# A hybrid attention and state-space block: PE's instruction order gets a rule on the kind of product, and attention's output gates are computed between heads and kept in DRAM

## The chip, the cores and the metric

The kernel runs on one core of a Trainium2 chip. The metric is device time in microseconds (us), the median of several executions. The core's engines are PE (matrix products), DVE (vector work), ACT (activations and copies), POOL, and SP, which here only issues transfers.

## The reference, cut to what matters

One encoder layer over 512 rows and 16 meta rows (L = 528), width 1024. Everything starts from one input projection; an attention branch of 16 heads and a state-space branch (SSD, 4 groups of 8 heads) run beside each other and are mixed by two gates.

```python
u = rmsnorm(h, norm_w[l])
proj = u @ w_in[l]
q_lat, kv_lat, k_rope, g_attn, z, xbc, dt_raw, merge = jnp.split(proj, offsets, axis=-1)
y_a = mla_branch(q_lat, kv_lat, k_rope, cos, sin, ...)        # 16 heads of softmax(q k^T) v
y_a = (y_a * jax.nn.silu(g_attn)) @ w_attn_proj[l]
y_s = ssd_branch(z, xbc, dt_raw, ...)                          # two directions, chunks of 128
y_s = y_s @ w_ssd_proj[l]
gates = jax.nn.sigmoid(merge).reshape(Bz, L, N_BRANCHES, D_MODEL)
mixed = gates[:, :, 0] * y_a + gates[:, :, 1] * y_s
h = h + mixed @ w_out[l]
h = rmsnorm(h, final_norm_w)
```

All inputs are float32. `gates[:, :, 0]`, the gate on attention's output, needs only `u` and 1024 columns of `w_in`.

## The kernel before, in words

The work is cut into small generators (units). A unit of the input projection loads a weight block of 1024 x 128 (512 KB, tile `wr`), ACT casts it to the high part `wh`, DVE makes the low part `wl`, and PE adds 24 products of 128x512 (or 48 of 128x270) into a PSUM tile `pj`: eight of high by high, eight of high by low, eight of low by high. That is the fp32r kind of product, one pass each. The SSD products (`st`, `yo`, `yd`, `cb` and a few more) take plain float32 operands, which PE runs as two recorded instructions each; the code calls these `four`. Transposes (`tr`, `yt`, `pt`) do not count as `four`.

PSUM has four one-bank tiles of tag "m" and two two-bank tiles of tag "d". The conv tiles of SSD, the products `yo`, attention's scores `sc` and keys take a "d" tile; each is handed back by DVE or ACT when it has been read.

Two steps set the order. First `drive` runs the units (main ones, and a queue of fillers, each with a condition) and records every operation with its place. Then `_Recorder.order` emits the operations by list scheduling: each engine has a clock, each operation an estimated length, and of all operations whose inputs are there the one with the earliest start, and among equals the one with the lowest place (`rank`), goes next. Each engine executes its own list strictly in that order. When PE goes from `four` to the other kind or back, this planner adds `SWITCH` = 95 ns.

```python
if o.eng == "PE" and o.four != four:
    four, more = o.four, self.SWITCH
```

For a head pair p of attention the queue holds the query and key units (`qst`, `kst`), values (`v`), the merge gate of the state-space branch (`merge_s`, tiles `ms`), and the branch gate `g` (`silu_tile`, tiles `z`). For a head, `score_gen` makes the scores `sc` in four row tiles; DVE takes the maximum `mx`, ACT the exponential `p`, DVE the reciprocal `sm` and the scaling; `value_gen` transposes (`pt`), splits into high (ACT) and low (DVE) parts `pT`, and multiplies with `v` into `o`. `split_y` splits the gated result `y` into `yah` and `yal`.

Attention's output gate is `merge_a(m)`, eight units of 24 products, each followed by one tanh on ACT into a tile `ma` of [128, 512]. Before, all eight may start when head 13 is done (`GATES` = 13), their tiles stay in SBUF, and `mix_unit(m)` uses them: it multiplies `ysp` (all eight split `y`) with `w_attn_proj`, then takes gate and sum. Behind the mixes come the last products `wo`.

Of the kernel before, what the change touches and what calls it, by code (L numbers as in the profile page):

```python
# [9 lines left out]
F32 = mybir.dt.float32  # L10
# [6 lines left out]
P = 128  # L17
# [26 lines left out]
LAG = 1250.0  # L44
MAHEAD, TOKC, CBC = 2, 2, 1
MAINS, OPEN, LOOK = 24, 4, 20
QLATE, GATES, SPLIT = 1, 13, 99


WPOOL, WPOOLB = 2, 4  # L50
# [41 lines left out]
class _Recorder:  # L92
# [15 lines left out]
    @classmethod  # L108
    def region(cls, ap):
        step = ap.ap[0][0]  # L110
        if ap.name == "cum_rows":
            return 0, 1, [(0, 1)]
        p0, f0 = divmod(ap.offset, step) if step else (0, ap.offset)
        dims = [(st, n) for st, n in ap.ap[1:] if st and n > 1]
        if "PSUM" in str(getattr(ap, "space", "")):
            end = f0 + sum(st * (n - 1) for st, n in dims)
            return 0, P, [(f0 // cls.BANK * cls.BANK, (end // cls.BANK + 1) * cls.BANK)]
        dims.sort(reverse=True)
        spans = [(f0, f0 + 1)]
        for k, (st, n) in enumerate(dims):  # L120
            rest = sum(a * (b - 1) for a, b in dims[k:]) + 1
            inner = sum(a * (b - 1) for a, b in dims[k + 1:]) + 1
            if inner >= st or n * len(spans) > 32:
                return p0, p0 + ap.shape[0], [(a, a + rest) for a, _ in spans]
            spans = [(a + st * m, a + st * m + 1) for a, _ in spans for m in range(n)]
        return p0, p0 + ap.shape[0], spans
# [31 lines left out]
        o.tiles = sorted({n for n, _ in rs + ws if n in self.tags})  # L158
        self.ops.append(o)

    AHEAD, SPARE = 4, 2
    TO_PE, TO_REST, SWITCH = 155.0, 35.0, 95.0

    def order(self):


        ops = self.ops
        left, ready = [0] * len(ops), [0.0] * len(ops)
        for o in ops:
            o.succs = []  # L170
        for o in ops:
            for k in o.preds:
                ops[k].succs.append(o)
            left[o.i] = len(o.preds)
        count, last, held, place, turn, passed = {}, {}, set(), {}, {}, {}
        for o in ops:
            for n in o.tiles:
                if n not in count:
                    tag = self.tags[n]
                    place[n] = turn.get(tag, 0)  # L180
                    turn[tag] = place[n] + 1
                count[n] = count.get(n, 0) + 1
        turn = {t: 0 for t in turn}
        passed = {t: set() for t in turn}
        free = {t: [0.0] * self.cap[t] for t in turn}
        clk = {e: 0.0 for e in ("PE", "DVE", "ACT", "POOL", "SP")}
        cand = {e: [] for e in clk}
        port = lock = wire = 0.0
        four = False
        for o in ops:  # L190
            if not left[o.i]:
                cand[o.eng].append(o)

        def when(o):
            t = max(clk[o.eng], ready[o.i], lock if o.eng == "POOL" else port if o.both else 0.0)
            for n in o.tiles:
                if n not in held:
                    tag = self.tags[n]
                    f, ahead = free[tag], place[n] - turn[tag]
                    if not f or ahead > self.AHEAD or (ahead > 0 and len(f) <= self.SPARE):  # L200
                        return None
                    t = max(t, f[0])
            return t

        out = []
        while len(out) < len(ops):
            best = None
            for q in cand.values():
                for o in q:
                    t = when(o)  # L210
                    if t is not None and (best is None or (t, o.rank) < best[:2]):
                        best = (t, o.rank, o)
            if best is None:
                raise RuntimeError(("no operation can go", len(out)))
            t, _, o = best
            cand[o.eng].remove(o)
            o.start = t
            for n in o.tiles:
                if n not in held:
                    held.add(n)  # L220
                    tag = self.tags[n]
                    free[tag].pop(0)
                    passed[tag].add(place[n])
                    while turn[tag] in passed[tag]:
                        turn[tag] += 1
            more = 0.0
            if o.eng == "PE" and o.four != four:
                four, more = o.four, self.SWITCH
            elif o.both:
                lock = t + o.occ  # L230
            elif o.eng == "POOL":
                port = t + o.occ + 60.0
            if o.eng == "SP":
                clk["SP"] = t + 420.0
                wire = max(wire, t + 1600.0) + o.dur
                end = wire + o.extra
            else:
                clk[o.eng] = t + o.occ + more
                end = t + o.dur + more
            for n in o.tiles:  # L240
                last[n] = max(last.get(n, 0.0), end + 40.0)
                count[n] -= 1
                if not count[n]:
                    f = free[self.tags[n]]
                    f.append(last[n])
                    f.sort()
            for s in o.succs:
                to = end + (self.TO_PE if s.eng == "PE" else self.TO_REST) if s.preds[o.i] else t + o.occ
                ready[s.i] = max(ready[s.i], to)
                left[s.i] -= 1  # L250
                if not left[s.i]:
                    cand[s.eng].append(s)
            out.append(o)
        self.span = max(o.start + o.dur for o in out)
        return sorted(out, key=lambda o: (o.start, o.i))
# [98 lines left out]
def hybrid_block_kernel(ctx, tc, a, out):  # L354
    nc = tc.nc
    scr = nc.dram_tensor("cum_rows", (2, NC, 32, P), F32, kind="Internal").ap()

    cp = ctx.enter_context(tc.tile_pool(name="cp", bufs=1))
    rp = ctx.enter_context(tc.tile_pool(name="rp", bufs=WRAW))
# [438 lines left out]
    def has(*keys):  # L798
        return lambda: all(k in done for k in keys)
# [468 lines left out]
    def merge_s(m):  # L1268
        w = yield from w_cols(O_MS + m * P)
        ps = yield from proj(w, u_src, QRY)  # L1270
        wdone()
        yield
        z = slot([P, NX], name="ms")
        A.activation(z, ps, AF.Tanh, scale=0.5)
        drop("m")
        yield
        V.scalar_tensor_tensor(ysacc[:, m, :], z, 1.0, ysacc[:, m, :], op0=ALU.add, op1=ALU.mult)
        done.add(("ms", m))

    w_ap = a["w_attn_proj"][0].rearrange("(k p) m -> p k m", p=P)  # L1280
    mx_, gates, ysp = {}, {}, {}

    def merge_a(m):
        w = yield from w_cols(O_MA + m * P)
        ps = yield from proj(w, u_src, QRY)
        wdone()
        yield
        z = slot([P, NX], name="ma")
        A.activation(z, ps, AF.Tanh, scale=0.5)
        drop("m")  # L1290
        gates[m] = z
        done.add(("ga", m))

    def split_y(p):
# [7 lines left out]

    def mix_unit(m):
        w = yield from weights(lambda raw: [(raw, w_ap[:, :, m * P:(m + 1) * P])], KD, P)
        ps = yield from proj(w, [ysp[p] for p in range(KD)], slice(0, NX))
        wdone()
        yield has(("ga", m), ("ms", m))
        z = gates.pop(m)
        V.scalar_tensor_tensor(z, z, 1.0, ps, op0=ALU.add, op1=ALU.mult)
        drop("m")  # L1310
        tt(V, z, z, ysacc[:, m, :], ALU.add)
        yield
        h = slot([P, NX], F32R, name="mxh")
        l = slot([P, NX], F32R, name="mxl")
        A.copy(h, z)
        yield
        lo_of(V, l, z, h)
        mx_[m] = (h, l)
        done.add(("mx", m))
# [117 lines left out]
    def fill(makes, cond=None):  # L1437
        for mk in makes:
            queue.append(Item(mk, cond))
# [85 lines left out]
    for p in range(KD):  # L1525
        if p % 2 == 0:
            fill([lambda p=p: pe_unit(p // 2)], lambda p=p: lat_ok() and score_ok(2 * p - 3))
        fill([lambda p=p: q_unit(p), lambda p=p: k_unit(p)], lambda p=p: "att" in done and lat_ok() and score_ok(2 * p - 2))
        if p % 2 == 0:
            fill([lambda p=p: v_unit(p // 2)], lambda p=p: lat_ok() and (p == 0 or ("A", 2 * p - 3) in done))  # L1530
        if p == 0:
            proj_fill(3)
        fill([lambda p=p: merge_s(p)], lambda p=p: ("proj", 3, p // 2) in done)
        if p + 1 < KD:
            g_fill(p + 1)
    fill([lambda m=m: merge_a(m) for m in range(KD)], lambda: ("A", GATES) in done)
    for h in range(NH):
        main(lambda h=h: score_gen(h), lambda h=h: ("q", h) in done and ("k", h) in done
             and (h < 1 or ("P", h - 1) in done) and (h < 2 or ("A", h - 2) in done))
# [47 lines left out]
```

## Time and profile before

| | |
|---|---|
| median of 3 runs | 912.46 us (910.71 to 915.15) |
| the profiled execution, its own time | 913.33 us |
| its span, first to last instruction | 911.5 us |
| PE busy | 878.5 us, 96% of the span |
| DVE busy | 707.9 us, 78% |
| ACT busy | 543.2 us, 60% |
| PE's idle time | 33 us |

Busy time of PE is the union of its matrix products; weight loads run beside them (PEld). The span falls into the start (to 25 us), the state-space groups (to about 500 us), attention's heads (to about 804 us), the mixes with the last products (to about 907 us) and the final rows. All work on `L261` is recorded by one helper, so instructions are told apart by their tiles.

### The profile page before, as it was taken

The page shows a single profiled execution, that of the slowest core. Times are in us where ns is not written, and L with a number is a line of the kernel's source. Part 1 is how long each engine was busy: PE and PEld are TensorE (multiplying, and loading weights), DVE is VectorE, ACT ScalarE, POOL GpSimd, SP SyncE. Part 2 cuts the span into 40 slices and gives each one's busy share as a digit, 9 for nine tenths or more (in the row PEclk, how much of TensorE's full clock was granted, in tenths as well). Part 3 has the DMA queues.
Part 4 walks back from the last instruction along what each step waited for, and adds up shares of the span by engine and source line. Part 5 has one row for each costly group of instructions (what it writes and reads, how often), then busy time and mean ns, then how long its engine had stood idle before and what let it go on. Part 6 is the DMA issues. An engine that isn't in the chain of part 4 may idle for free.

```text
span 911.5 us, 13243 instructions
## 1 busy us (share of the span) xinstructions
PE 878.5 (96%) x4984; PEld 725.7 (80%) x4984; DVE 707.9 (78%) x1245; ACT 543.2 (60%) x1159; POOL 11.7 (1%) x20
## 2 busy tenths in 40 slices
PE   7999999999989999999999999999999999999997
PEld 5997878867878769977788888877777878888885
DVE  6798799968799689979768757969989897334464
ACT  6369469965776447855344556757777685432232
POOL 1000000000000000000001000000000000000000
PEclk9999999999999999999999999999999999999998
DMA  7254246434524236332224333121121001433322
GB/s 219 71 165 119 70 120 166 109 93 113 141 70 139 70 84 160 104 116 70 70 70 102 81 87 92 38 53 29 38 50 33 15 24 47 135 121 101 104 70 92
DMA packets 126952, 83.30 MB, mean 91 GB/s; under 512 B 26354, under 2 KB 114071, under 8 KB 126889
## 3 DMA queue, kind: packets, MB, share of 16 engines
q1 hardware_dynamic: 126709, 82.33, 33.3%
q8 instruction: 39, 0.64, 0.3%
q14 instruction: 24, 0.20, 0.1%
q10 hardware_dynamic: 180, 0.14, 0.0%
HBM read 80.22 MB, written 2.23 MB: 90 GB/s over the span
## 4 chain that ended last, share of the span: by engine, by line
PE 74%; DVE 17%; ACT 4%; issue 2%; DMA 1%; POOL 0%; POOLq 0%; ACTq 0%; DVEq 0%
PE pj L261 53%; PE wo L261 4%; PE sc L261 3%; PE st L261 2%; PE yo L261 2%; PE o L261 2%; DVE x L261 2%; DVE wl L261 2%; PE pt L261 2%; PE tr L261 2%; PE yd L261 1%; DVE mx L261 1%; DVE pT L261 1%; DVE yo L261 1%; DVE C L261 1%
## 5 line engine op out<-in xcount | busy, mean ns | idle before, releaser
L261 PE MATMUL pj<-uh,wh 128*128 128x512 f32 (+3 forms) x776 | 158.8, 346 | 8.0 <-DVE yo L261 3.5
L261 DVE TENSOR_TENSOR wl<-wr,wh 128x1024 fp32r<-128x1024 f32 (+1 forms) x102 | 123.9, 1217 | 53.2 <-ACT wh L261 53.0
L261 PE MATMUL pj<-uh,wl 128*128 128x270 f32 (+3 forms) x776 | 157.1, 339 | 0.0
L261 PE MATMUL pj<-ul,wh 128*128 128x270 f32 (+3 forms) x776 | 150.0, 335 | 0.0
L261 ACT CAST wh<-wr 128x1024 fp32r<-128x1024 f32 (+1 forms) x102 | 106.3, 1042 | 63.1 <-PE pj L261 41.3
L261 PEld LDWEIGHTS pj<-uh,wh 128*128 128x128 f32 (+1 forms) x776 | 121.9, 191 | 27.6 <-issue 5.1
L261 PEld LDWEIGHTS pj<-ul,wh 128*128 128x128 f32 (+1 forms) x776 | 122.6, 189 | 15.0
L261 PEld LDWEIGHTS pj<-uh,wl 128*128 128x128 f32 (+1 forms) x776 | 122.0, 190 | 13.2 <-issue 0.2
L261 ACT ACTIVATE ar<-ar,nacs 128x128 f32<-128x128 f32 x256 | 80.8, 391 | 24.5 <-DMA ar<-cum_rows 19.3
L261 PE MATMUL sc<-kst,qst 96*128 96x264 f32 (+1 forms) x384 | 67.2, 299 | 6.3 <-ACT p L261 5.4
L261 PEld LDWEIGHTS sc<-kst,qst 96*128 96x128 f32 (+1 forms) x384 | 53.6, 189 | 11.7 <-ACT p L261 8.6
L261 ACT ACTIVATE p<-sc,mx 128x528 f32<-128x528 f32 x64 | 45.3, 707 | 21.3 <-DVE mx L261 20.8
L261 PE MATMUL pt<-cst,p 128*128 128x128 f32 (+1 forms) x320 | 52.2, 274 | 1.4 <-DVE pT L261 0.8
L261 DVE TENSOR_TENSOR pT<-pt,pT 128x512 fp32r<-128x512 f32 x64 | 43.8, 685 | 11.5 <-ACT pT L261 11.3
L261 PE MATMUL o<-pT,v 128*128 128x512 f32 x128 | 46.6, 417 | 3.5 <-ACT pT L261 2.9
L261 DVE SCALAR_TENSOR_TENSOR x<-pj,chv,x 128x528 f32<-128x528 f32 x64 | 48.8, 763 | 0.8 <-ACT x L261 0.3
L261 PEld LDWEIGHTS pt<-cst,p 128*128 128x128 f32 (+1 forms) x320 | 37.3, 130 | 12.7 <-DVE p L261 1.5
L261 DVE TENSOR_REDUCE mx<-sc 128x1 f32<-128x528 f32 x64 | 44.6, 698 | 2.2 <-PE sc L261 1.9
L261 ACT CAST pT<-pt 128x512 fp32r<-128x512 f32 x64 | 37.3, 587 | 14.6 <-PE pt L261 14.4
L261 ACT ACTIVATE w<-cbm,dt_t 128x128 f32<-128x128 f32 x128 | 39.9, 390 | 2.9 <-DVE cbm L261 2.9
L261 PE MATMUL pj<-nh,wh 128*128 128x512 f32 x128 | 39.6, 431 | 0.0
L261 DVE SCALAR_TENSOR_TENSOR w<-cbm,dt_t,w 128x128 f32<-128x128 f32 x128 | 38.1, 347 | 0.0
(224 smaller groups left out, 1467.2 us busy)
## 6 DMA issues: line engine op xcount, KB each, us to landing
wr<-in_w_in SPq DMA_DIRECT2D x69, 512.0 KB, 4.0
ar<-cum_rows SPq DMA_DIRECT2D x32, 512.0 KB, 5.3
wr<-in_w_ssd_proj SPq DMA_DIRECT2D x16, 512.0 KB, 3.4
wr<-in_w_attn_proj SPq DMA_DIRECT2D x8, 512.0 KB, 3.6
wr<-in_w_out SPq DMA_DIRECT2D x8, 512.0 KB, 3.7
ws<-in_w_uq SPq DMA_DIRECT2D x36, 64.0 KB, 3.3
xt<-in_x SPq DMA_DIRECT2D x4, 512.0 KB, 5.3
fin<-in_x SPq DMA_DIRECT2D x4, 512.0 KB, 6.0
```

What stands on the lines that cost most here:

```text
L261: o.fn(*o.args, **o.kw)
```

## The change: what it does

There are two parts. In `order`, a PE operation of the other kind than the one PE last ran gets 30 added to its place when candidates with the same start are compared (`STAY`). And `merge_a(p - 1)` is queued with head pair p, to start when head 2p-1 is done (the last one when head 14 is done); its tile goes to DRAM (`gate_rows`) by a transfer on SP's queue, and `mix_unit` loads it back into a tile `ga` before its products.

```diff
-QLATE, GATES, SPLIT = 1, 13, 99
+QLATE, SPLIT = 1, 99
...
-    AHEAD, SPARE = 4, 2
+    AHEAD, SPARE, STAY = 4, 2, 30
...
                     t = when(o)
-                    if t is not None and (best is None or (t, o.rank) < best[:2]):
-                        best = (t, o.rank, o)
+                    if t is None:
+                        continue
+                    r = o.rank + (self.STAY if o.eng == "PE" and o.four != four else 0)
+                    if best is None or (t, r) < best[:2]:
+                        best = (t, r, o)
...
+    gate_scr = nc.dram_tensor("gate_rows", (KD, P, NX), F32, kind="Internal").ap()
...
     def merge_a(m):
         w = yield from w_cols(O_MA + m * P)
...
         z = slot([P, NX], name="ma")
         A.activation(z, ps, AF.Tanh, scale=0.5)
         drop("m")
-        gates[m] = z
+        yield
+        S.dma_start(gate_scr[m], z)
         done.add(("ga", m))
...
     def mix_unit(m):
         w = yield from weights(lambda raw: [(raw, w_ap[:, :, m * P:(m + 1) * P])], KD, P)
+        yield has(("ga", m))
+        z = slot([P, NX], name="ga")
+        S.dma_start(z, gate_scr[m])
         ps = yield from proj(w, [ysp[p] for p in range(KD)], slice(0, NX))
         wdone()
-        yield has(("ga", m), ("ms", m))
-        z = gates.pop(m)
+        yield has(("ms", m))
...
         fill([lambda p=p: merge_s(p)], lambda p=p: ("proj", 3, p // 2) in done)
+        if p:
+            fill([lambda p=p: merge_a(p - 1)], lambda p=p: ("A", 2 * p - 1) in done)
         if p + 1 < KD:
             g_fill(p + 1)
-    fill([lambda m=m: merge_a(m) for m in range(KD)], lambda: ("A", GATES) in done)
+    fill([lambda: merge_a(KD - 1)], lambda: ("A", NH - 2) in done)
```

The order that comes out differs on PE, DVE, ACT and SP from about the second state-space step on. PE's list shows it at three places (the number behind a name is its buffer, the same tile may have another number in the other kernel).

The first place is PE's list at the beginning of the first state-space group; `st` are the float32 products of the states. Before:

```order
L261 MATMUL st_225<-xw_224,bt_193 128x512
L261 MATMUL tr_227<-cst,x_81_185 16x128 x4
L261 MATMUL pj_237<-uh,wh_230 128x512 x8
L261 MATMUL pj_237<-uh,wl_231 128x512 x4
L261 MATMUL st_238<-xw_235,bm_198 128x512
L261 MATMUL tr_240<-cst,x_81_185 128x128 x4
L261 MATMUL pj_237<-uh,wl_231 128x512 x4
L261 MATMUL pj_237<-ul,wh_230 128x512 x8
L261 MATMUL st_243<-xw_242,bt_193 128x512
L261 MATMUL tr_245<-cst,x_81_185 128x128 x4
```

The same place in the change:

```order
L266 MATMUL tr_227<-cst,x_81_185 16x128 x4
L266 MATMUL st_225<-xw_224,bt_193 128x512
L266 MATMUL pj_237<-uh,wh_230 128x512 x8
L266 MATMUL pj_237<-uh,wl_231 128x512 x4
L266 MATMUL tr_240<-cst,x_81_185 128x128 x4
L266 MATMUL pj_237<-uh,wl_231 128x512 x4
L266 MATMUL pj_237<-ul,wh_230 128x512 x8
L266 MATMUL tr_245<-cst,x_81_185 128x128 x4
L266 MATMUL pj_249<-uh,wh_233 128x270
L266 MATMUL st_238<-xw_235,bm_198 128x512
L266 MATMUL st_243<-xw_242,bt_193 128x512
```

The second and the third `st` have moved behind the transposes and the rest of the unit, and stand together.

The second place is PE's list between two heads in the middle of attention, beginning within the scores of one row tile. Before:

```order
L261 MATMUL sc_1230<-kst_812,qst_811 128x264
L261 MATMUL o_1192<-pT_1214,v_1134 128x512
L261 MATMUL sc_1230<-kst_812,qst_811 128x264 x4
L261 MATMUL o_1192<-pT_1214,v_1134 128x512
L261 MATMUL pt_1234<-cst,p_1201 128x128 x2
L261 MATMUL pt_1226<-cst,p_1212 128x128
L261 MATMUL pt_1234<-cst,p_1212 128x128
L261 MATMUL sc_1236<-kst_812,qst_811 128x264 x3
L261 MATMUL o_1192<-last_821,v_1145 128x512
L261 MATMUL sc_1236<-kst_812,qst_811 128x264 x3
```

The matching place in the change, where `pj_1257` is a unit of `merge_a`:

```order
L266 MATMUL sc_1251<-kst_812,qst_811 128x264 x3
L266 MATMUL o_1211<-pT_1232,v_1162 128x512
L266 MATMUL sc_1251<-kst_812,qst_811 128x264 x3
L266 MATMUL pj_1257<-uh,wh_1252 128x512 x2
L266 MATMUL pt_1247<-cst,p_1234 128x128
L266 MATMUL pj_1257<-uh,wh_1252 128x512 x2
L266 MATMUL o_1211<-last_821,v_1166 128x512
L266 MATMUL pj_1257<-uh,wh_1252 128x512 x3
L266 MATMUL pt_1247<-cst,p_1234 128x128
L266 MATMUL pj_1257<-uh,wh_1252 128x512
L266 MATMUL pj_1257<-uh,wl_1253 128x512 x4
```

The holes between transposes, scores and `o` now have the products of a gate unit in them.

The third place is PE's list where the last head ends. Before, with `pj_1402` and `pj_1415` as units of `merge_a`:

```order
L261 MATMUL pj_1402<-uh,wh_1391 128x512 x8
L261 MATMUL pj_1402<-uh,wl_1392 128x512 x4
L261 MATMUL o_1384<-pT_1398,v_1252 128x512 x2
L261 MATMUL pt_1403<-cst,p_1359 16x128 x2
L261 MATMUL pt_1403<-cst,p_1372 16x128 x2
L261 MATMUL pj_1402<-uh,wl_1392 128x512 x4
L261 MATMUL pj_1402<-ul,wh_1391 128x512 x8
L261 MATMUL o_1384<-pT_1400,v_1255 128x512 x2
L261 MATMUL o_1384<-last_821,v_1266 128x512
L261 MATMUL pj_1415<-uh,wh_1405 128x512 x8
L261 MATMUL pj_1415<-uh,wl_1406 128x512 x8
```

The same place in the change, where `pj_1430` is the first mix and waits for `yah`:

```order
L266 MATMUL o_1399<-pT_1406,v_1275 128x512 x2
L266 MATMUL pt_1410<-cst,p_1384 128x128 x2
L266 MATMUL pt_1410<-cst,p_1395 128x128 x2
L266 MATMUL pt_1412<-cst,p_1384 16x128 x2
L266 MATMUL pt_1412<-cst,p_1395 16x128 x2
L266 MATMUL o_1399<-pT_1408,v_1287 128x512
L266 MATMUL pj_1430<-yah_1350,wh_1423 128x512
L266 MATMUL o_1399<-pT_1408,v_1287 128x512
L266 MATMUL o_1399<-pT_1411,v_1296 128x512
L266 MATMUL pj_1430<-yah_1352,wh_1423 128x512
L266 MATMUL o_1399<-pT_1411,v_1296 128x512
L266 MATMUL pj_1430<-yah_1354,wh_1423 128x512
```

The gate units behind the last head are gone; the first mix begins with the seven `yah` that are ready.

## Rows read from the trace of the kernel before

**Rows 1.** The page: busy time, and the granted clock in 40 slices.

```profile
PE 878.5 (96%) x4984; PEld 725.7 (80%) x4984; DVE 707.9 (78%) x1245; ACT 543.2 (60%) x1159; POOL 11.7 (1%) x20
...
PEclk9999999999999999999999999999999999999998
```

**Rows 2.** Busy time by stage; columns: stretch, its length, each engine's busy time (instructions).

```profile
110.00:500.00 390.00, 382.38 (x2235) 311.22 (x2234) 335.99 (x567) 245.99 (x563) 6.54 (x7) 1.00 0.39 105
500.00:560.00 60.00, 60.00 (x314) 50.59 (x312) 40.22 (x74) 32.19 (x63) 0.00 (x0) 1.00 0.35 87
560.00:760.00 200.00, 188.01 (x1144) 157.72 (x1143) 174.94 (x356) 144.99 (x311) 0.00 (x0) 1.00 0.18 40
760.00:880.00 120.00, 120.00 (x550) 97.71 (x549) 55.05 (x74) 41.95 (x62) 0.00 (x0) 1.00 0.32 101
```

**Rows 3.** PE's waits: us in total, times, longest.

```profile
PE sc L261 <- ACT p L261: 5.4, 9, 1.4
PE pj L261 <- DVE yo L261: 3.5, 2, 2.0
...
PE pj L261 <- DVE x L261: 2.8, 2, 2.1
...
PE nwb L261 <- DMA nw<-in_norm_w: 2.2, 1, 2.2
```

**Rows 4.** The chain that ended last, 200 to 232 us: start, us, what.

```profile
200.97 1.73 PE yo L261 x4
...
209.89 1.02 PE yd L261 x16
210.92 1.91 PE yo L261 x4
212.83 2.78 PE pj L261 x12
215.61 0.86 PE st L261 x2
...
216.90 5.57 PE pj L261 x24
222.47 0.59 PE yd L261 x8
...
231.11 1.05 PE st L261 x2
```

**Rows 5.** Busy time in six stretches between heads, with their sum.

```profile
567.00:573.10 6.10, 4.54 (x30) 3.65 (x30) 6.10 (x14) 4.47 (x11) 0.00 (x0) 1.00 0.00 0
...
730.00:736.40 6.40, 4.96 (x28) 3.15 (x26) 6.20 (x14) 5.49 (x14) 0.00 (x0) 1.00 0.32 82
sum 38.70, PE 29.48 PEld 22.20 DVE 37.72 ACT 31.15 POOL 0.00; mean PE 4.91 PEld 3.70 DVE 6.29 ACT 5.19 POOL 0.00
```

**Rows 6.** Busy time in a stretch with a gate `g` as filler.

```profile
658.00:668.00 10.00, 9.43 (x51) 7.62 (x51) 7.12 (x16) 5.66 (x14) 0.00 (x0) 1.00 0.01 2
```

**Rows 7.** Busy time during PE's wait at 116 us and just after it.

```profile
116.10:118.10 2.00, 0.02 (x1) 0.00 (x0) 2.00 (x5) 0.33 (x2) 0.00 (x0) 1.00 0.66 149
118.10:121.90 3.80, 3.80 (x18) 3.80 (x19) 3.80 (x7) 0.61 (x1) 0.00 (x0) 0.55 0.88 260
```

**Rows 8.** The timeline where the last head ends: start, us, engine, what.

```profile
798.36 1.23 DVE L261 TENSOR_TENSOR wl<-wr,wh 128x1024 fp32r<-128x1024 f32 x1 [3.03 <-ACT wh L261]
...
804.42 0.39 PE L261 MATMUL o<-last,v 128*128 128x512 f32 x1
...
805.72 0.58 ACT L261 COPY y<-o 64x512 f32<-64x512 f32 x1
...
806.99 0.69 DVE L261 TENSOR_TENSOR y<-o,y 64x512 f32<-64x512 f32 x1
...
808.44 0.62 ACT L261 CAST yah<-y 128x512 fp32r<-128x512 f32 x1 [2.14 <-DVE y L261]
```

**Rows 9.** Transfers by line: count, KB each, median us to landing.

```profile
out<-fo SPq DMA_DIRECT2D x8, 256.0 KB, 2.2
```

More of the change, by code (lines that the diff above doesn't have):

```diff
@@ L112, in region @@
             return 0, 1, [(0, 1)]
+        if ap.name == "gate_rows":
+            return 0, 1, [(ap.offset // (P * NX), ap.offset // (P * NX) + 1)]
         p0, f0 = divmod(ap.offset, step) if step else (0, ap.offset)
@@ L1280, in hybrid_block_kernel @@
     w_ap = a["w_attn_proj"][0].rearrange("(k p) m -> p k m", p=P)
-    mx_, gates, ysp = {}, {}, {}
+    mx_, ysp = {}, {}
     def merge_a(m):
```

## The prediction, made before the change was run

> **What bounds the kernel now.** I read the page first. PE is busy 96% of the span at full clock nearly throughout, DVE 78% [rows 1], so the end comes earlier only if PE does less or waits less. The change takes no product away: both lists of PE hold the same 4744 products. So the question is where PE's 33 us of idle time lie. The table by stage answers it [rows 2]: from 500 to 560 us and from 760 to 880 us PE never idles; from 110 to 500 us it idles 390 - 382.4 = 7.6 us; from 560 to 760 us, the middle of attention, 200 - 188.0 = 12.0 us. The rest lies at the start and in the last rows, which the change does not touch.
>
> PE's waits say what ends these holes [rows 3]. In attention it is the softmax chain (`sc` waits for the exponential, which hands the "d" tile back, 9 times, 5.4 us). Among the state-space groups a conv unit waits for a "d" tile that DVE still reads (`yo`, `x`: four waits, 6.3 us). PE waits for a transfer only once, at the start, so a load issued somewhat later has cover.
>
> In attention the holes sit in one kind of place. Six stretches between heads, 38.7 us together, have PE busy 29.48 us, so 9.2 us idle; DVE is busy 37.72 us there, 97% [rows 5]. In those stretches no filler unit is left. With a gate `g` as filler, from 658 us, PE idles 0.57 us of 10 and DVE is at 71% [rows 6]. The other 161.3 us of the 200 hold only 12.0 - 9.2 = 2.8 us, or 1.7%.
>
> **The change, part one: STAY.** The planner believes that each change between float32 products and the rest costs 95 ns, and the new rule avoids such changes. Counting in the two lists, there are 119 before and 81 after, 38 fewer. The chain prices them [rows 4]: twelve products `pj` start at 212.83 and take 2.78, so the two recorded `st` start at 215.61, exactly behind them, and take 0.86, as two passes do. Four recorded `yo` behind `pj` take 1.73 us. Nothing is lost in these changes, so 38 x 0 = 0.
>
> `yd` alone differs. Its outputs fill 64 columns of the array. Sixteen take 1.02 us, eight 0.59, so eight more cost 0.43 and 0.16 is lost on entering; behind it four `yo` take 1.91 instead of 1.73 and two `st` 1.05 instead of 0.86, so 0.18 to 0.19 is lost on leaving [rows 4]. A visit to `yd` costs 0.35 us beyond its products. The lists have 25 visits before and 26 after: +0.35 us.
>
> The Trainium skill, TensorEngine Tiling (Array Packing), section Key Properties, says that a change of the tiling mode drains the engine. The trace agrees as far as `yd` goes, the only product here on half the columns: it pays 0.35 us a visit, and a change of the number format alone pays nothing. By that page the flag `four` marks the wrong thing, and the sum would again be +0.35.
>
> What is left of part one is that it moves things. In a group's beginning, two `st` of the state chain now come after the rest of a unit, some twelve products or 2.8 us later, and DVE gets the states later. DVE is busy 336 of 390 us in that stage [rows 2], so idling it there can come back as a wait of PE. The price of one such event is seen at 116 us: PE idles 2.0 us while DVE is busy throughout, and in the 3.8 us after it the granted clock is 0.55 on average, which is mostly the lower level of 1.2 GHz, and that costs 3.8 x 0.45 = 1.7 us [rows 7]. So one event costs 2.0 to 3.7 us. The stage could lose this one (-3.7), or win another (+3.7). At the site itself DVE has the same operations to do before it hands the tile back, and it is the one that is late, so I expect the wait to stay; I take +0.5 for the whole stage and keep -3.7 and +3.7 as bounds.
>
> **Part two: the gates between heads.** A gate unit is 24 products, 5.57 us of PE [rows 4], and 1.23 us of DVE for `wl` [rows 8]. Six of eight move from behind head 13 to the holes between heads, the other two into the last two heads. The order shows them cut into ones to fives, between exactly those transposes, scores and `o` that waited.
>
> The six stretches would then hold 29.48 + 6 x 5.57 = 62.9 us of PE work and 37.72 + 6 x 1.23 = 45.1 us of DVE work. PE is the longer now, so the idle share should fall from 24% to that of stretches with filler. That is 1.7% on average and 5.7% in the one shown; I take 3%, or 1.9 us of 64.8. Saved: 9.2 - 1.9 = 7.3 us, in bounds of 0 (the holes stay) and 12.0 (all idle time of 560 to 760 us gone).
>
> Two things are given back. Heads 14 and 15 had six gate units among them and no idle time at all from 760 us on; with less filler the 22 us of work that stay run at the 3%: +0.7. And nothing is left behind the last head except the mixes, which need its `y`. Before, from the last `o` at 804.42 to the end of `yah` at 809.06 us it took 4.64 us [rows 8], hidden under gate units. Some 0.9 us of that was ACT busy with a weight cast (the copy starts at 805.72 though the product ended at 804.81), so 3.7 remain. The new order puts 4 + 7 products of the first two mixes there, 11 x 0.23 = 2.6 us, beside the `o` itself, 0.2. Uncovered: +1.0 (bounds 0 and 3.7).
>
> The transfers cost nothing by this sum. Eight gates of 256 KB go out and eight come back; the kernel's transfers of that size, `fo` to the output, land in 2.2 us [rows 9]. A write waits on SP for its tanh, and the weight loads queued behind it wait too, but PE waited for no load in attention [rows 3], and the gates come back while the mix before them runs, 24 products or 5.57 us. If that cover were gone, each late one would cost up to its 2.2.
>
> **The sum.** 0 (kinds) + 0.35 (`yd`) + 0.5 (groups) - 7.3 (holes) + 0.7 (last heads) + 1.0 (the end) = -4.75 us. The profiled execution took 913.33, 0.87 above the median of the runs. So 908.6 against it, and against the median 907.7.
>
> **The rivals.**
> - The holes move and do not close. PE executes in order, so a block of four to twelve gate products also holds up the next link of the softmax chain by 0.9 to 2.8 us, and DVE at 97% in the old holes speaks for a chain that sets its own pace. Against it: with `g` as filler the idle share is 5.7%, a quarter of that in the holes. If half of the 7.3 is lost so, the time is 907.7 + 3.7 = 911.4.
> - The wait at 116 us goes: a half-clock spell and the wait less, 907.7 - 0.5 - 3.7 = 903.5. For it: the products ahead of it are regrouped. Against it: DVE's amount of work there.
> - The changes of kind do cost what the planner says: 38 x 0.095 = 3.6 us more are saved: 904.1. The chain speaks against it.
> - Slower: the late states make DVE late in each group. The price is an event like that at 116 us, 3.7 us; without any the sum is 907.7 - 0.5 = 907.2. To reach 917, 0.5% above the median, takes 9.8 us or three events, which in four groups of the same form is possible: 907.2 + 11.1 = 918.3. For it: DVE is busy 86% there and four waits of PE already end on DVE. Against it: the order of DVE's list changes little, and only by neighbours.
>
> **How the numbers follow.** The forecast has 0.44 (its own range, from the share of the holes that close, 905 to 910), the holes that move 0.28, the wait that goes 0.12, the kinds 0.06, slower 0.10. About 0.5%, or 4.6 us, is what a measurement of this kernel can tell from no change, so faster means below 907.9 and slower above 917.0. Faster is somewhat over half of the forecast and the two cases near 904: 0.48. Same is the rest of the forecast and the holes that move: 0.42. Slower 0.10. The range from 902 to 914 leaves out the slow case and the tails of the others.
>
> **What would show it.** Right: PE's idle time from head 2 to head 13 falls from 12 us to about 5, and the waits of `sc` for `p` shrink; one or two short waits appear behind the last head; `st` behind `pj` still costs nothing; `yd` has 26 visits. Wrong: idle time in attention near 8 us or more, waits of `pj` for `x` or `yo` above the 6.3 us in the groups, a second spell of the lower clock, or PE waiting for a transfer in the mixes.

## The result

The changed kernel takes 902.0 us (median of 4 runs, 901.0 to 903.35), the kernel before 912.48 (4 runs); the ratio is 0.9884, 95% interval 0.9856 to 0.9911. That is 10.5 us less, faster by more than the 0.5% that a measurement can tell. The forecast of 907.7 had the direction, but 4.75 us where 10.5 were saved; its range ends at the measured median.

The page of the changed kernel, the lines that answer to [rows 1]:

```profile
span 901.6 us, 13284 instructions
PE 877.7 (97%) x4984; PEld 724.0 (80%) x4984; DVE 708.9 (79%) x1245; ACT 544.0 (60%) x1159; POOL 12.6 (1%) x20
PEclk9999999999999999999999999999999999999998
```

PE is idle for 901.6 - 877.7 = 23.9 us instead of 33.0, so 9.1 of the 9.9 us by which the span is shorter are idle time. The stages of [rows 2] in the changed kernel:

```profile
110.00:500.00 390.00, 382.44 (x2224) 308.63 (x2223) 332.47 (x562) 246.10 (x563) 7.52 (x7) 1.00 0.37 103
500.00:560.00 60.00, 59.55 (x315) 50.11 (x314) 42.76 (x79) 31.51 (x63) 0.00 (x0) 1.00 0.42 106
560.00:760.00 200.00, 199.35 (x1180) 169.67 (x1179) 164.92 (x326) 140.56 (x293) 0.00 (x0) 1.00 0.23 57
760.00:880.00 120.00, 117.77 (x567) 94.87 (x566) 74.37 (x118) 53.21 (x91) 0.00 (x0) 1.00 0.34 110
```

In the middle of attention the idle time is down from 12.0 to 0.65 us. From 760 us on there are now 2.2 us where there were none, and the groups keep theirs (7.6 both times). PE's waits from 25 to 880 us, what waits, for what, us in total, times, the longest:

```profile
PE pj L266 <- DVE x L266: 2.5, 2, 1.8
PE pj L266 <- DVE yo L266: 2.2, 2, 2.0
PE pj L266 <- ACT wh L266: 1.9, 1, 1.9
PE pj L266 <- DVE pT L266: 1.0, 2, 0.9
...
PE sc L266 <- DVE qst L266: 0.5, 1, 0.5
...
PE sc L266 <- ACT p L266: 0.2, 1, 0.2
```

`sc` waits for `p` once instead of nine times [rows 3], and no row names a transfer. The wait of [rows 7] stayed, and so did the half-clock stretch behind it, at 0.51 of full clock, which is nearly all at 1.2 of 2.4 GHz:

```profile
116.30:118.30 2.00, 0.25 (x2) 0.26 (x3) 2.00 (x4) 0.09 (x1) 0.00 (x0) 1.00 0.81 219
118.50:121.90 3.40, 3.40 (x18) 3.40 (x17) 3.40 (x7) 0.99 (x3) 0.00 (x0) 0.51 0.93 261
```

The end of the last head, on PE alone (start, us, what, and in brackets the idle time before it):

```profile
803.94 0.50 PE L266 MATMUL pj<-yah,wh 128*128 128x512 f32 x1 [0.87 <-DVE pT L266]
...
805.43 0.39 PE L266 MATMUL o<-last,v 128*128 128x512 f32 x1
805.66 2.71 PE L266 MATMUL pj<-yah,wh 128*128 128x512 f32 x11
808.60 0.50 PE L266 MATMUL pj<-yah,wh 128*128 128x512 f32 x1 [0.22 <-ACT yah L266]
```

Eleven products of the first two mixes stand there, as foreseen, and cover all but 0.22 us of the wait for `yah`.

### The profile page after: what moved, and what is told of

It is laid out like the page before. It is cut to its first block, busy times and chain, and to the rows that moved or that the text cites. A ratio compares the mean times of both kernels' runs of the same rounds, so it can differ in the third digit from the quotient of the medians.

```text
span 901.6 us, 13284 instructions
## 1 busy us (share of the span) xinstructions
PE 877.7 (97%) x4984; PEld 724.0 (80%) x4984; DVE 708.9 (79%) x1245; ACT 544.0 (60%) x1159; POOL 12.6 (1%) x20
## 4 chain that ended last, share of the span: by engine, by line
PE 54%; DVE 6%; ACT 3%; issue 1%; POOL 0%; POOLq 0%; ACTq 0%; DVEq 0%
PE pj L266 35%; PE sc L266 4%; PE wo L266 4%; PE pt L266 3%; PE o L266 3%; PE v L266 1%; PE yo L266 1%; DVE wl L266 1%; PE yd L266 1%; PE st L266 1%; DVE pT L266 1%; DVE w L266 1%; DVE yo L266 1%; ACT p L266 1%; DVE mx L266 0%
## 5 line engine op out<-in xcount | busy, mean ns | idle before, releaser
L266 PE MATMUL pj<-uh,wh 128*128 128x512 f32 (+3 forms) x776 | 161.7, 346 | 7.1 <-DVE x L266 2.5
L266 PE MATMUL pj<-uh,wl 128*128 128x270 f32 (+3 forms) x776 | 159.4, 340 | 0.0
L266 PE MATMUL pj<-ul,wh 128*128 128x270 f32 (+3 forms) x776 | 152.2, 337 | 0.0
L266 PE MATMUL sc<-kst,qst 96*128 96x264 f32 (+1 forms) x384 | 65.1, 297 | 1.2 <-DVE qst L266 0.5
L266 PE MATMUL o<-pT,v 128*128 128x512 f32 x128 | 44.5, 406 | 0.4 <-DVE pT L266 0.4
```

The source lines that it names most:

```text
L266: o.fn(*o.args, **o.kw)
```

## The experiments

Ratios are to the kernel before on the same chip, with 95% intervals. The rule of the diff is called STAY, part two the gates.

**The two parts apart.** STAY alone, in the kernel before:

```diff
-    AHEAD, SPARE = 4, 2
+    AHEAD, SPARE, STAY = 4, 2, 30
...
+                    r = o.rank + (self.STAY if o.eng == "PE" and o.four != four else 0)
```

> The kernel before with STAY = 30 alone; the gates stay behind head 13 in SBUF. Holes theory (the moved gates earned all of the gain, the rule on kinds moves things without a price): 912 to 913.5 us, idle time of PE near 12 us from 560 to 760 us and near 7.6 from 110 to 500, 81 changes of kind at no cost, 26 visits to yd (+0.35). Kinds theory (each of the 38 changes saved is worth the 95 ns of SWITCH): 912.5 - 3.6 = 908.9 us, busy time of PE 3.6 us lower.

Measured: 915.38, ratio 1.0031 [1.0018, 1.0044]. STAY alone makes the kernel 2.8 us slower, slower than either theory said. The 38 fewer changes of kind bring nothing.

The gates alone, in the changed kernel:

```diff
-    AHEAD, SPARE, STAY = 4, 2, 30
+    AHEAD, SPARE, STAY = 4, 2, 0
```

> The changed kernel with STAY = 0: gates between heads and in DRAM, the old rule on ties. Holes theory: 901.5 to 903 us, PE idle under 1.5 us from 560 to 760 us. Kinds theory: 902 + 3.6 = 905.6 us, and busy time of PE higher by that.

Measured: 898.64, ratio 0.9853 [0.9833, 0.9873], 14.1 us less than before and 3.4 less than the whole change, and less than either theory said. The gates carry all of the gain.

The trip through DRAM alone: the gates go out and come back, but start behind head 13 as before, without STAY.

```diff
+        S.dma_start(gate_scr[m], z)
...
+        S.dma_start(z, gate_scr[m])
...
-    fill([lambda m=m: merge_a(m) for m in range(KD)], lambda: ("A", GATES) in done)
+    fill([lambda m=m: merge_a(m) for m in range(KD)], lambda: ("A", 13) in done)
```

> The kernel before with nothing but the round trip: all eight gate units may start after head 13 as before, the gate goes to DRAM and is loaded back by the mix, STAY = 0. Holes theory: the transfers are hidden, 912.5 us within 1 us, idle time from 560 to 760 us stays near 12 us. Rival (the freed SBUF tiles earn part of the gain): below 910 us.

Measured: 913.57, ratio 1.0009 [0.9994, 1.0023]. The sixteen transfers are hidden, and what the gates gain comes from their place. The holes are as they were, PE 188.38 of 200 us:

```profile
560.00:760.00 200.00, 188.38 (x1142) 157.88 (x1141) 174.33 (x353) 144.64 (x309) 0.00 (x0) 1.00 0.17 38
```

**Half of the holes.** Three gates between heads (units 1, 3 and 5), five behind head 13, STAY = 0:

```diff
-        if p:
+        if p in (2, 4, 6):
...
-    fill([lambda: merge_a(KD - 1)], lambda: ("A", NH - 2) in done)
+    fill([lambda m=m: merge_a(m) for m in (0, 2, 4, 6, 7)], lambda: ("A", 13) in done)
```

> Gates only (STAY = 0), but three of the eight units between heads (1, 3 and 5) and five after head 13. Holes theory with a fixed worth of a hole (11.3 us over six holes, 1.9 each): 912.5 - 3 x 1.9 = 906.8 us, and three holes left of the six. Rival (what counts is that PE has more work than DVE over the whole of attention, so that gaps anywhere close together): closer to 902 than to 912, 903 to 905 us.

Measured: 907.63, ratio 0.9954 [0.9939, 0.9969]. PE is busy 192.99 us of the 200, nearly midway between 188.0 and 199.3, and `sc` waits for `p` for the holes that are left:

```profile
PE sc L266 <- ACT p L266: 3.5, 6, 1.4
PE pj L266 <- ACT yah L266: 1.6, 1, 1.6
```

So three of the six holes give 5.0 of the 11.3 us of idle time that all six give, near what the first theory expected. The end takes some back: `pj` waits 1.6 us for `yah`, against 0.2 with the whole set of gates.

**The end.** The last two gates kept for the last head, STAY = 0:

```diff
-            fill([lambda p=p: merge_a(p - 1)], lambda p=p: ("A", 2 * p - 1) in done)
+            fill([lambda p=p: merge_a(p - 1)], lambda p=p: ("A", 2 * p - 1 + (p == KD - 1)) in done)
...
-    fill([lambda: merge_a(KD - 1)], lambda: ("A", NH - 2) in done)
+    fill([lambda: merge_a(KD - 1)], lambda: ("P", NH - 1) in done)
```

> Gates alone (STAY = 0), with the last two gate units kept for the last head: unit 6 from head 14 on, unit 7 only when head 15's probabilities are done. If the uncovered end behind the last head costs about 1 us, as the prediction says, the last wait before the mixes goes and the time is 897.5 to 898.2 us; if the holes of head 14 open instead, 898.6 to 900 us.

Measured: 903.45, ratio 0.9890 [0.9871, 0.9909], 4.8 us worse than the gates alone and slower than both ranges expected. The holes of head 14 open again and the wait at the end is longer, not gone; from 760 us on PE idles 4.2 us instead of 2.2:

```profile
PE pj L266 <- ACT yah L266: 1.6, 1, 1.6
PE sc L266 <- ACT p L266: 1.1, 2, 1.0
```

From the product where the two lists part to the last `wo` it takes 343.3 us instead of 340.8, so 2.5 of the 4.8 us lie there. Its executions also have a lower mean granted clock, 0.994 against 0.995.

**What STAY costs.** First by direction: with the gates, only float32 products are held back, or only the others.

```diff
-                    r = o.rank + (self.STAY if o.eng == "PE" and o.four != four else 0)
+                    r = o.rank + (self.STAY if o.eng == "PE" and o.four and not four else 0)
```

```diff
-                    r = o.rank + (self.STAY if o.eng == "PE" and o.four != four else 0)
+                    r = o.rank + (self.STAY if o.eng == "PE" and four and not o.four else 0)
```

> The changed kernel, but the 30 places are added only to float32 products while PE is on the other kind (99 changes of kind, 26 visits to yd); the rest is never held back. Late-states theory (STAY costs because st, yo and yd come later and DVE with them): it carries the whole cost, 902 us within 1. Rival (the cost lies in holding the projections back, or in the mere reshuffle at attention's start): 899 to 900 us, near the gates alone at 898.6.

> The mirror image: only the other kinds are held back while PE is on float32 products (105 changes of kind, 26 visits to yd), so no st, yo or yd comes later than without the rule. Late-states theory: 898.6 us within 1, as with the gates alone. Rival: 901 to 902 us.

Measured: 900.31, ratio 0.9857 [0.9839, 0.9875], and 900.33, ratio 0.9855 [0.9836, 0.9873]. Neither differs from the gates alone by more than the intervals. Late states, which only the first of them has, do not carry the price by themselves.

Then by stage: STAY only in the groups, and only behind them (the second has `>=`).

```diff
+            products += o.eng == "PE"
...
-                    r = o.rank + (self.STAY if o.eng == "PE" and o.four != four else 0)
+                    r = o.rank + (self.STAY if o.eng == "PE" and o.four != four and products < 2470 else 0)
```

> The changed kernel with STAY = 30 in force only until PE's list has 2470 of its 4744 products, which is just behind the last yd; nothing held back later. Where does STAY's price lie? Theory one, in the state-space groups: the time is that of the whole change, 902.0 (ratio to before 0.988). Theory two, at attention's start, where STAY regroups rb, ssq and pj (32 rows of PE's list differ there): the time is that of the gates alone, 898.6 to 899.5 (0.985). A share of each lies between, 900 to 901.

> The mirror: STAY = 30 in force only from the 2470th product of PE's list on. Theory one (the groups carry the price): 898.6 to 899.5, as the gates alone (0.985). Theory two (attention's start carries it): 902.0 (0.988).

Measured: 899.49, ratio 0.9855 [0.9834, 0.9876], and 899.66, ratio 0.9859 [0.9838, 0.9881]. Again each alone is within the intervals of the gates alone, so each half by itself says that the price lies in the other. So the whole change was run beside the gates alone on one chip, both kernels unaltered:

> The whole change, unaltered, beside the gates alone on the same chip. What STAY costs on top of the gates is open: the medians of different sets of runs differ by 902.0 - 898.6 = 3.4 us, but STAY in the groups alone came to 899.5 and STAY behind them alone to 899.7, 0.9 and 1.0 us above the gates alone. Theory one, the price adds up and is that of STAY without the gates (+2.8): 2.5 to 3.5 us above e16_gates, ratio to before near 0.988. Theory two, with the gates it is the sum of the two parts, +1.9, or less: 0 to 2 us above e16_gates, ratio 0.985 to 0.987.

> The gates alone (STAY = 0), beside e15_whole on the same chip: both theories 898 to 900, ratio to before 0.985; what counts is the distance to e15_whole.

Measured: 901.78, ratio 0.9876 [0.9855, 0.9897], against 900.46, ratio 0.9857 [0.9839, 0.9875]. The distance is 1.3 us; with the first pair it is between 1.3 and 3.4. On top of the gates STAY's price is about as large as the intervals, so the halves could not be told apart by these times. The traces are sharper. Two groups of the first 500 us, without STAY (gates alone), then with it (the whole change): the group, its count, and behind the bar PE's busy time, the mean in ns, the idle time.

```profile
L266 PE MATMUL pj<-ul,wh 128*128 128x270 f32 (+3 forms) x600 | 105.7, 318 | 0.0
L266 PE MATMUL yo<-h,C 128*128 128x512 f32 x56 | 27.6, 609 | 0.0
```

```profile
L266 PE MATMUL pj<-ul,wh 128*128 128x270 f32 (+3 forms) x600 | 107.9, 320 | 0.0
L266 PE MATMUL yo<-h,C 128*128 128x512 f32 x56 | 29.0, 616 | 0.2
```

The kernel before has 105.7 and 27.6 as well; STAY alone has 107.6 and 29.0, STAY in the groups alone 107.7 and 29.0. So where STAY acts in the groups, the same products take 3.3 to 3.6 us more of PE's busy time in these two groups (others give back a part). Behind the groups it adds one wait, `sc` for `qst`, 0.5 us: from 500 to 560 us PE is busy 59.5 us with STAY there and 60.00 without.

The medians hide this price because the clock differs between the sets of runs: the mean granted clock is 0.998 for STAY in the groups alone and 0.995 for the gates alone. Some profiled executions have no half-clock stretch like that of [rows 7] before the last rows, and these can be compared directly. Each stretch here runs from the 501st to the 3143rd record of PE (about 84 to 550 us), which is the same set of products in every list. The columns are those of [rows 2]. First the half of the holes, whose list is up to there that of the kernel before; then STAY in the groups alone, STAY alone, and a run that follows below, the kernel before with only `yd` held back:

```profile
83.70:547.65 463.95, 456.63 (x2643) 371.52 (x2642) 386.20 (x653) 285.37 (x639) 6.54 (x7) 1.00 0.38 102
84.62:550.95 466.33, 458.65 (x2644) 371.57 (x2642) 385.85 (x653) 285.85 (x639) 7.53 (x7) 1.00 0.37 102
84.84:551.56 466.72, 459.44 (x2644) 371.34 (x2642) 385.96 (x653) 285.29 (x639) 7.52 (x7) 1.00 0.38 102
84.60:545.35 460.75, 454.08 (x2644) 372.65 (x2642) 386.09 (x653) 284.79 (x639) 7.93 (x7) 1.00 0.38 103
```

STAY takes 2.4 us more in the groups and 2.8 us with the wait for `qst`, nearly all of it as busy time of PE. So its price lies in the groups for the greater part. With only the float32 products held back, again without a half-clock stretch, the same stretch takes 464.95 us, 1.0 more than without the rule. These are single executions; two whose lists are alike there but for a few places behind the groups (the second line and the third) differ by 0.4 us.

**What a change of the array's mode costs.** The flag `four` now marks only products on 64 columns, which is `yd`, and the planner is told that such a change costs 175 ns:

```diff
-    AHEAD, SPARE, STAY = 4, 2, 30
-    TO_PE, TO_REST, SWITCH = 155.0, 35.0, 95.0
+    AHEAD, SPARE, STAY = 4, 2, 60
+    TO_PE, TO_REST, SWITCH = 155.0, 35.0, 175.0
...
-                         four=self.name == "PE" and op != "transpose" and not kw.get("is_transpose") and lhs.dtype == F32)
+                         four=self.name == "PE" and op != "transpose" and not kw.get("is_transpose") and lhs.dtype == F32 and cols == 64)
```

> The changed kernel with the kinds drawn elsewhere: only products with 64 output columns (yd) are a kind of their own, STAY = 60, SWITCH = 175 ns. Visits to yd fall from 25 (gates alone) to 15. Drain theory (a visit costs 0.34 us beyond its products, and number formats nothing): 898.6 - 10 x 0.34 = 895.2 us, and busy time of PE some 3 us lower. Rival (holding yd back makes DVE late, which hands x back later): the gain is eaten, 898 to 901 us.

Measured: 895.16 (894.09 to 895.49), ratio 0.9797 [0.9784, 0.9811]. With ten visits fewer than the gates alone it is 3.5 to 5.3 us faster (898.64 and 900.46 without), of which the clock has a part: its executions have a mean granted clock of 0.998, the gates alone 0.995. It is the fastest version of all, 6.8 us below the change as made.

The same rule in the kernel before, gates unmoved:

> The kernel before, gates where they were, with only yd held back: the flag four marks products with 64 output columns alone, STAY = 60, SWITCH = 175. The list then has 15 visits to yd in place of 25. Drain theory, 0.35 us a visit and independent of the gates: 10 x 0.35 = 3.5 us less than before, 909.1 to 910.1 (ratio 0.9955 to 0.997). Rival, that e5_s60 gained because it and the gates helped each other in attention: no difference from before, 0.999 to 1.001.

Measured: 908.81, ratio 0.9959 [0.9944, 0.9975]: 4.1 us for ten visits, or 0.41 each (0.23 to 0.51 by the interval). It does not need the gates. Here too the clock has a part, 0.998 against 0.995 in the runs of the kernel before. Between the same products, without a half-clock stretch, it is 463.95 - 460.75 = 3.2 us, or 0.32 a visit (the first and the last of the four lines above); with the gates the stretch takes 460.59 us. `yd` and the `yo` that often follows it, in the first 500 us, before and then with this rule:

```profile
L261 PE MATMUL yo<-h,C 128*128 128x512 f32 x56 | 27.6, 609 | 0.0
L261 PE MATMUL yd<-w,xtk 128*64 128x128 f32 x256 | 19.7, 282 | 0.0
```

```profile
L266 PE MATMUL yo<-h,C 128*128 128x512 f32 x56 | 26.7, 593 | 0.0
L266 PE MATMUL yd<-w,xtk 128*64 128x128 f32 x256 | 18.1, 279 | 0.0
```

The same 256 products take 1.6 us less for ten entries, 0.16 each, and 0.9 of the loss on leaving is seen in `yo`.

A stronger hold, with the gates:

```diff
-    AHEAD, SPARE, STAY = 4, 2, 60
+    AHEAD, SPARE, STAY = 4, 2, 200
```

> The version with gates between heads and yd alone held back, STAY = 200 in place of 60: 11 visits to yd in place of 15. Drain theory: 4 x 0.35 = 1.4 us less than the 895.2 of STAY = 60, so 893.8 (ratio 0.978). Rival, that DVE gets yd's results so late that it holds up a tile: 896 to 899, with waits of PE for yo or x longer than the 2 us each has now.

Measured: 897.33, ratio 0.9833 [0.9812, 0.9854], slower than STAY = 60 though it has four visits fewer. The waits are those of the rival: `pj` waits 3.0 us for `yo` and 2.2 us for `x`, where STAY = 60 has 1.5 and 1.6, and from 84 to 547 us PE idles 8.6 us instead of 6.5. That eats up the four visits; the rest of the 2.2 us goes with the clock, 0.996 against 0.998, since the profiled execution has a half-clock stretch that the one of STAY = 60 does not have.

```profile
PE pj L266 <- DVE yo L266: 3.0, 2, 2.4
PE pj L266 <- DVE x L266: 2.2, 4, 0.8
```

## Why the prediction was right and wrong, point by point

Five profiled executions, with idle time as span less busy time, carry most of it:

| | span | PE busy | idle |
|---|---|---|---|
| before | 911.5 | 878.5 | 33.0 |
| STAY alone | 912.9 | 879.6 | 33.3 |
| gates alone | 897.3 | 874.6 | 22.7 |
| the change | 901.6 | 877.7 | 23.9 |
| gates, `yd` held back | 892.3 | 869.4 | 22.9 |

**Changes of kind: right.** Their term was 0, and STAY alone, with 38 fewer, has no less busy time. In the changed kernel float32 products behind the others still start without a loss: eight `pj`, two `st`, two `yo`.

```profile
198.01 2.01 PE L266 MATMUL pj<-ul,wh 128*128 128x512 f32 x8
199.87 1.02 PE L266 MATMUL st<-xw,bt 128*128 128x512 f32 x2
200.72 1.02 PE L266 MATMUL yo<-h,C 128*128 128x512 f32 x2
```

`yo` starts 0.85 us behind `st`, which is two `st` at their usual pace [rows 4]. The rival by which kinds cost 95 ns falls. That `yd` alone differs is not quite right, though. The `st` on 16 rows pay too, in the kernel before:

```profile
187.31 1.09 PE L261 MATMUL pj<-uh,wl 128*128 128x512 f32 x4
188.34 1.12 PE L261 MATMUL st<-xw,bm 16*128 16x512 f32 x2
189.39 0.66 PE L261 MATMUL tr<-cst,x 128*128 128x128 f32 x4
```

The four `pj` ahead take 1.03 us instead of 0.93 and the two `st` 1.05 instead of 0.86. These four pairs stand in both lists, so no term of the sum changes by it.

**A visit to `yd`: right in price, about 0.35.** Taking ten away measured 0.41 each by the medians without the gates, and 0.32 where the clock was alike. What the Trainium skill says in TensorEngine Tiling (Array Packing), section Key Properties, of a drain at a change of tiling mode, agrees with these runs; they add the price.

**The groups, +0.5: too small.** With `yd` the forecast gave STAY +0.85; STAY alone measured +2.8, on top of the gates +1.3 to +3.4. No event of 2.0 to 3.7 us appeared and the wait at 116 us stayed, so the step looked for the loss in the wrong form: it is spread over `yo` and `pj` as longer busy time of the same products, with idle time up by only 0.3. Neither direction nor stage alone shows it beyond the intervals of the medians; between the same products at the same clock it is 2.4 us in the groups, and 2.8 with the wait for `qst`. One visit more, 0.35, is a part of it. Why `yo` and `pj` take longer stays open. It is known only that five `yd` visits now hand over to `pj<-ul,wh`, which then pays the loss on leaving.

**The holes, -7.3: right in mechanism, too small by half.** This is the step that failed. For the gates alone, the forecast's terms are -7.3 + 0.7 + 1.0 = -5.6; measured is -14.1 (and -13.5 in the second pair). Two sizes were off. First, the remaining idle time was taken as 3% of the six stretches, 1.9 us, and the other stretches' 2.8 us were left as they were; in the trace all of 560 to 760 us keeps 0.66 us, so 11.3 us of idle time went, close to the bound of 12.0. The stretch with `g` from which the 3% was reasoned [rows 6] has its filler mostly in blocks of 7 and 12 products, while the gate units stand in the old holes in pieces of one to five as well. That this is why they close more is argued, not shown.

Second, and missing from the working altogether: the busy time that the six stretches showed was not all work. A product's record lasts longer than the time it adds, since the next one starts inside its tail. In a hole nothing does, and the tail counts as busy. The scores and transposes of the changed kernel, without a hole:

```profile
568.63 0.60 PE L266 MATMUL pt<-cst,p 128*128 128x128 f32 x4
568.98 0.98 PE L266 MATMUL sc<-kst,qst 96*128 96x264 f32 x6
569.80 0.62 PE L266 MATMUL o<-pT,v 128*128 128x512 f32 x2
570.26 0.60 PE L266 MATMUL pt<-cst,p 128*128 128x128 f32 x4
```

Four `pt` last 0.60, but `sc` starts after 0.35; six `sc` last 0.98, `o` starts after 0.82; two `o` last 0.62, `pt` starts after 0.46. So by these records 0.16 to 0.25 us of each tail lie beside the next product. Before a wait they lie beside nothing. The same attention products from 480 to 880 us, before and then with the gates alone:

```profile
L261 PE MATMUL o<-pT,v 128*128 128x512 f32 x128 | 46.6, 417 | 3.5 <-ACT pT L261 2.9 <-DVE pT L261 0.6
L261 PE MATMUL pt<-cst,p 128*128 128x128 f32 x256 | 42.4, 275 | 1.4 <-DVE pT L261 0.8 <-DVE p L261 0.5
L261 PE MATMUL sc<-kst,qst 128*128 128x264 f32 x192 | 35.1, 301 | 4.2 <-ACT p L261 4.0
L261 PE MATMUL o<-last,v 128*128 128x512 f32 x16 | 6.9, 433 | 0.6 <-DVE last L261 0.6
```

```profile
L266 PE MATMUL o<-pT,v 128*128 128x512 f32 x128 | 44.6, 406 | 0.4 <-DVE pT L266 0.4
L266 PE MATMUL pt<-cst,p 128*128 128x128 f32 x256 | 41.2, 273 | 0.3 <-DVE p L266 0.2
L266 PE MATMUL sc<-kst,qst 128*128 128x264 f32 x192 | 33.0, 298 | 0.2 <-ACT p L266 0.2
L266 PE MATMUL o<-last,v 128*128 128x512 f32 x16 | 6.3, 394 | 0.0
```

The counts are equal, and the sum falls from 131.0 to 125.1, 5.9 us that stood under "busy" (the two groups left out, `sc` on 96 rows and the last `pt` on 16 columns, have 42.0 and 42.1). Such sums count a tail twice where another product runs beside it. The whole of PE, from the product where the two lists part to the last `wo`, which is the same set of products, gives the net figures, before and then with the gates alone:

```profile
550.41:904.74 354.33, 342.33 (x1845) 283.12 (x1843) 249.75 (x465) 201.86 (x402) 1.66 (x3) 1.00 0.23 63
549.71:890.56 340.85, 337.95 (x1845) 281.57 (x1843) 251.07 (x465) 203.26 (x402) 1.67 (x3) 1.00 0.27 78
```

The stretch is 13.5 us shorter, 9.1 by idle time (12.0 to 2.9: the 11.3 less 2.2 at the end) and 4.4 by busy time. That is the 13.5 to 14.1 of the medians. So the holes themselves gave 15.7 us where 7.3 were forecast, 11.3 shown as idle time and 4.4 hidden as busy. The waits of PE that the profile lists from 480 to 880 us fall from 24 to 9; 15 tails of 0.16 to 0.25 us make 2.4 to 3.8 us of the 4.4, and the rest may be waits too short to reach beyond a tail, which is not shown.

**The last heads and the end, +0.7 and +1.0: nearly right.** From 760 to 880 us 2.2 us of idle time appeared, 1.7 was said. Keeping two gates back for the end made it worse.

**The transfers, 0: right.** The trip alone measured 1.0009 [0.9994, 1.0023].

**The rivals.** The holes closed, they did not move. The wait at 116 us did not go. The slower case had its mechanism wrong but its sign is that of STAY alone. That the median still came to the end of the range is luck in part: the gates gave some 8 us more than their terms, and STAY took 1.3 to 3.4 us back where 0.85 was forecast.

## What to carry to other kernels

Idle time is a lower bound of what a hole costs: add the tail of the product ahead of each wait, here some 0.2 us each. Filler that can be cut between the links of a chain closed nearly all of it here. Ask of a rule in a planner which cost of the chip it stands for; here the number format cost nothing and the count of columns did, and the same rule on the right products is worth 3.2 us where the one on the wrong ones cost 2.4 to 2.8, both between the same products at the same clock. Test the parts of a change apart, since here one part hid a loss in the other's gain; and where a price is as large as the scatter, compare the same products in executions with the same clock.

## What the runs showed of the hardware that was not expected

Entering products on 64 columns and leaving them again costs 0.32 to 0.41 us of PE (ten visits fewer, 3.2 us by the rows and 4.1 by the medians), and a pair of `st` on 16 rows loses about 0.3, while a change between float32 and fp32r products on 128 rows and 128 columns costs nothing that a row shows. And executions of one kernel differ along with their mean granted clock: of the eleven of the trip through DRAM, the four at 0.996 and 0.997 took 910.4 to 912.5 us, the seven at 0.993 to 0.995 took 912.3 to 915.9. A difference of 1 to 2 us between two kernels can be one of the clock; of the 4.1 us above, 0.9 is more than the rows show.
